# Attention scores on two halves of the rows, S5 in crosswise groups, another order at the ends of the MLPs, and a retuned schedule

## The chip, the cores and the metric

One core of one Trainium2 chip. The metric is the device time of one execution in microseconds. Three executions of the kernel before took 1063.42, 1063.46 and 1065.54 us; the median is 1063.46.

## The reference, cut to what matters

Two residual layers on x of 512 tokens by 1024, float32, each followed by a squared-ReLU MLP (1024 to 4096 and back), every part with an RMS norm ahead and behind. Layer 0 mixes by S5 (32 groups of 16 channels, 64 complex states) and by attention with forget gates (8 heads of 64); layer 1 by pooling and by a spatial gating unit.

```python
def s5_mixer(u, lam_re, lam_im, log_dt, b_re, b_im, c_re, c_im, d, w_glu):
    ...                                   # a = exp(lam dt), bb = q b
    bu = einsum('lbgh,gph->lbgp', ut, bb)             # complex
    x = associative_scan(x_t = a x_{t-1} + bu_t)      # over the tokens
    y = gelu(Re(x c) + d * u)
    return y * sigmoid(y @ w_glu)

def fox_attention(q, k, v, f_logit, b_f):
    F = cumsum(log_sigmoid(f_logit + b_f), axis=1)
    # per block i of 128 queries:
    s = einsum('bqhd,bkhd->bhqk', qi, k) * Dh ** -0.5 + (F_q - F_k)
    p = softmax(where(k_pos <= q_pos, s, -inf))
    return einsum('bhqk,bkhd->bqhd', p, v)

def sq_relu_mlp(h, w1, w2):
    return square(relu(h @ w1)) @ w2

for l in range(2):
    x = x + rms_norm(mixer_l(rms_norm(x)))
    x = x + rms_norm(sq_relu_mlp(rms_norm(x), w1[l], w2[l]))
```

## The kernel before

Every engine call is recorded by a `Program` (`record`), and at the end `issue` puts the recorded operations into an order for each engine: a list scheduler runs a model of the engines with costs from `cost`, and takes of the ready operations the one with the best priority. The priority comes from the place in the record and from labelled bonuses in the table `BOOST`; `LOOKS` and `RANK` set how far ahead of the oldest operation an engine may look, `STICKY` favours a bank of PSUM that is already being accumulated. Buffers and banks are given out in that order too. All recorded rows of the profile therefore carry one line, L438, and are told apart by their tiles: `b` is a working buffer, `bank` one of the eight banks of PSUM, `ct` the constants, `maskb` and `identb` the causal mask and the identity in bf16. The number behind a name is that of its allocation, and isn't the same in two kernels.

Products in float32 are made of parts: `split` writes a high part (fp32r, by ACT) and the rest (by DVE), and `mm3` multiplies high by high, rest by high and high by rest. A product of 128 rows, 128 outputs and 512 columns is the usual unit.

The mixer of layer 0 is recorded in the order of `ORDER`: f (forget gates), z c t o e (preparation of S5), q0 to q3 (q and k of a pair of heads), u (the S5 input), a0 to a3 (attention of a pair), s0 to s3 (a quarter of S5).

`qk_block` makes q and k of two heads: the product has head 0 on partitions 0 to 63 and head 1 on 64 to 127. Before, four buffers of 1024 columns are filled from it by half-height copies: Q1 and K1 hold for each head both parts stacked on 128 rows, Q2 and K2 the remaining part and, on other rows, the forget terms. `attention` then makes the scores of a head and block with two products of full height (the second 96 or 128 rows) and one product of mask with identity between. The softmax is on DVE and ACT, the probabilities are transposed, and the products with v go to two halves of the columns, one head on each. The blocks come in two phases: (0, 1) and (2, 3).

`step_z` transposes the S5 input matrices in quadrants of 64 x 64 (`ct,b 64*64 64x64` rows). `s5_run` takes a quarter (8 groups): 16 quadrant products W into two banks, complex rotation, two scans and back-rotation on DVE, then one T product and two S products per pair of groups.

The MLP's second product uses a seven-product scheme with the names S1 to S4, A22, X and Z (`Seven`). Its last step, `tail`, works for each half a of the tokens through four groups of 12 matmuls, by (Z, S4), (X, S2), (X, S3), (X, A22). X goes on accumulating while `collect` reads it in between, so the group behind has to wait for that read. When a tile of the output is complete, `post` normalises it, adds it to x, and norms and transposes it for the next layer.

At the start SP issues the loads in the recorded order up to `prog.first`, PE runs 16 warm-up matmuls on `idle`, and the first four tiles of x are normed (`norm_T`) one after another, with rstd computed by two small operations on POOL.

Of the kernel before, what the change touches and what calls it, by code (L numbers as in the profile page):

```python
# [36 lines left out]
LOOKS = {0: (202, 21, 10), 1: (186, 29, 7), 2: (48, 11, 15), 3: (36, 8, 6)}  # L37
HAMT = 3060
POOLF = 1
NWARM = 16  # L40
RANK = 0.55
# [3 lines left out]
PBOOST = 3  # L45
STICKY = 7
# [13 lines left out]
C_ID, C_SEL, C_MASK, C_TRIL, C_IPAD, C_DIAG, C_MISC, C_INV = 0, 128, 256, 384, 512, 736, 752, 768  # L60
C_END = 832


def constants(np):
# [19 lines left out]
    for hd in range(8):  # L84
        c[:, m + 5 + hd] = p % 32 // 4 == hd
    c[:, m + 13] = j >= 2
# [81 lines left out]
class Program:  # L168
# [10 lines left out]
    def __init__(self, engines):  # L179
        self.ops, self.engines, self.rooms = [], engines, []  # L180
        self.shift = 0
        self.boost = 0.0
        self.phase = 0
        self.first = 0

    def record(self, eng, name, args, kw):
# [12 lines left out]
        op.port = eng in ("DVE", "POOL") and name == "tensor_tensor" and not any(v.t.bank for v in ins)  # L199
        if eng == "PE":  # L200
# [6 lines left out]
            op.half = (p0, p0 + outs[0].shape[0]) if ins[0].shape[0] == 128 else (0, 128)  # L207
        for v in ins:
# [36 lines left out]
    def cost(eng, name, outs, ins, args, kw):  # L245
# [8 lines left out]
        if eng == "PE":  # L254
# [7 lines left out]
            if ins[0].t.dt == BF16 or out.shape[0] <= 64:  # L262
                return max(53, cols / 2.4 + 3)
            return max(107, cols / 2.4 + 15)
        if eng == "ACT":
            ptr = sum(isinstance(kw.get(k), View) for k in ("bias", "scale", "accum_out"))
            return 0.833 * n + (67 if psum else 93) + 90 * ptr
        if eng == "DVE":
# [8 lines left out]
            return (0.52 if fast else 1.04) * n + 67 + 64 * ptr  # L277
        if eng == "POOL":
# [4 lines left out]
            if name == "tensor_copy":  # L283
                return 0.83 * n + 180
            return 1.7 * n + 165 + 130 * (name == "tensor_scalar")
        if outs:
            v = outs[0]
            return v.shape[0] * free(v) * 4 / 270.0
        return 1600

    def issue(self):
# [43 lines left out]
        window, work, slow, half = 0, 0.0, 2.0, None  # L335
        events = []
# [19 lines left out]
        while len(order) < total:  # L356
            moved = True
            while moved:
                moved = False
                for e in self.engines:  # L360
# [3 lines left out]
                    for o in avail[e]:  # L364
                        if o.ready <= now and o.wake <= now and not (e == "SP" and head and o is not head[0]):
# [21 lines left out]
                    if e == "SP":  # L387
                        clock[e] = now + 60
                        dma = max(dma, now) + o.ns
                        o.end = dma + 2000  # L390
                    elif e == "PE":
# [3 lines left out]
                        ns = o.ns  # L395
                        if half is not None and (half[1] <= o.half[0] or o.half[1] <= half[0]):
# [145 lines left out]
def tile_trunk(ctx: ExitStack, tc: tile.TileContext, x, mix_pre_g, mix_post_g, mlp_pre_g, mlp_post_g,  # L542
# [431 lines left out]
    class Seven:  # L974
# [55 lines left out]
        def collect(self, row1, c, bank_, a, first=False):  # L1030
            kept = boosted(f"Y{prog.phase}")
# [68 lines left out]
        def tail(self, post, before):  # L1100
# [4 lines left out]
            parts = [[self.part(self.raw[p][1].f(512, 512)) for p in range(4)]]  # L1105
            for p in range(4):
                H, L = self.middle(p)
                parts.append([((H, L), (H.r(0, 512), L.r(0, 512))), ((H, L), (H.r(512, 512), L.r(512, 512)))])
            second, parts = parts[1:], parts[:1]
            parts.append([s_[0] for s_ in second])  # L1110
            parts.append([s_[1] for s_ in second])
            last = []
            for p in range(4):
                r1 = self.raw[p][1]
                last.append(self.part(r1.f(0, 512)))
                r1.free()
            parts.append(last)
# [860 lines left out]
```

## Time and profile before

| | us |
|---|---|
| median of three executions | 1063.46 |
| the profiled execution | 1063.45 |
| its span (first to last instruction) | 1061.7 |
| mean granted clock, as a share of full speed | 0.993 |
| POOL busy | 57.2 |
| DMA, mean over the span | 98 GB/s |

The time of an execution is 1.75 us longer than the span that its instructions take. Rows of the timeline read: start, busy time, engine, line, operation, out<-in, shapes, count, and in brackets the idle time ahead with the engine that ended it. A float32 product on part of the array leaves two records. Rows by group read: line, engine, operation, names and shapes, count, then busy time and mean ns of one, then idle time ahead with its releasers. The layers lie in time so: start to 25 us, layer 0's mixer to 215, its MLP to 585, layer 1's mixer to 730 and its MLP to the end.

### The profile page before, as it was taken

How to read it: one execution, taken by the hardware profiler on the slowest of the kernel's cores; microseconds unless marked ns; L12 is line 12 of the kernel's file. 1: busy time of each engine (PE TensorE's matmuls, PEld its weight loads, DVE VectorE, ACT ScalarE, POOL GpSimd, SP SyncE). 2: the span in 40 equal slices, each digit the busy share in tenths (PEclk: the TensorE clock that was granted, in tenths of full speed). 3: DMA queues.
4: the chain of work that ended last, by engine and by line, in shares of the span. 5: the costliest groups of instructions: out<-in, count | busy, mean ns of one | idle time of the engine just before them, and what ended most of it. 6: DMA issues, size and time to landing. Idle time of an engine off the chain costs nothing.

```text
span 1061.7 us, 13872 instructions
## 1 busy us (share of the span) xinstructions
PE 1039.3 (98%) x5133; PEld 846.6 (80%) x5133; DVE 792.9 (75%) x1365; ACT 568.5 (54%) x1037; POOL 57.2 (5%) x112
## 2 busy tenths in 40 slices
PE   8999899999999999999999799999999999999996
PEld 5789677788988888888888688889888888888885
DVE  6968899759856586677778998566776697686786
ACT  5474978546744563553653644445645544553641
POOL 4001000003000000000001310011000000000001
PEclk9999999999999999999999899999999999999999
DMA  8221012623314322422514533306134225223212
GB/s 254 68 80 40 2 40 81 218 60 119 120 40 131 120 72 66 143 85 78 160 60 132 156 100 113 106 4 198 39 99 121 98 80 164 75 80 120 79 59 80
DMA packets 110385, 104.53 MB, mean 98 GB/s; under 512 B 9736, under 2 KB 92844, under 8 KB 110318
## 3 DMA queue, kind: packets, MB, share of 16 engines
q1 hardware_dynamic: 110318, 103.66, 31.8%
q8 instruction: 40, 0.66, 0.3%
q14 instruction: 27, 0.22, 0.1%
HBM read 101.55 MB, written 2.10 MB: 98 GB/s over the span
## 4 chain that ended last, share of the span: by engine, by line
PE 89%; ACT 5%; DVE 2%; SPq 1%; issue 1%; POOL 1%; DMA 0%; DVEq 0%; POOLq 0%; ACTq 0%
PE bank L438 89%; ACT b L438 5%; DVE b L438 2%; SPq L438 1%; POOL small L438 1%; DMA b<-in_x_dram 0%; ACT junk L438 0%; DVE small L438 0%; POOL b L438 0%; DVEq L1974 0%; POOLq L1974 0%; ACTq L438 0%; ACTq L1974 0%; DVEq L438 0%; POOLq L438 0%
## 5 line engine op out<-in xcount | busy, mean ns | idle before, releaser
L438 PE MATMUL bank<-b,b 128*128 128x512 f32 (+5 forms) x4684 | 1000.2, 376 | 8.9 <-DVE b L438 8.0
L438 PEld LDWEIGHTS bank<-b,b 128*128 128x128 f32 (+2 forms) x4684 | 810.3, 188 | 182.3 <-DVE b L438 7.2
L438 DVE TENSOR_TENSOR b<-b,b 128x1024 fp32r<-128x1024 f32 (+7 forms) x654 | 483.2, 775 | 128.8 <-ACT b L438 65.2
L438 ACT ACTIVATE b<-b 128x1024 fp32r<-128x1024 f32 (+6 forms) x582 | 376.1, 690 | 261.3 <-DVE b L438 121.9
L438 ACT ACTIVATE b<-bank 128x512 f32<-128x512 f32 (+7 forms) x269 | 131.3, 516 | 148.4 <-PE bank L438 138.2
L438 DVE TENSOR_TENSOR b<-bank,b 128x512 f32<-128x512 f32 (+2 forms) x210 | 120.7, 604 | 50.9 <-PE bank L438 30.9
L438 DVE TENSOR_TENSOR b<-b 128x256 f32<-128x256 f32 (+5 forms) x202 | 91.0, 466 | 36.0 <-PE bank L438 23.9
L438 POOL TENSOR_SCALAR small<-small 128x1 f32<-128x1 f32 x36 | 15.9, 443 | 852.9 <-ACT junk L438 836.7
L438 ACT ACTIVATE junk<-b 128x512 bf16<-128x512 f32 (+1 forms) x32 | 27.0, 843 | 43.5 <-DVE b L438 37.0
L438 PE MATMUL bank<-ct,b 128*128 128x128 f32 (+3 forms) x387 | 43.0, 260 | 5.0 <-DVE b L438 4.5
L438 DVE SCALAR_TENSOR_TENSOR b<-b,small,b 128x1024 f32<-128x1024 f32 (+1 forms) x32 | 36.4, 1150 | 14.8 <-POOL small L438 14.8
L438 PEld LDWEIGHTS bank<-ct,b 128*128 128x128 f32 (+3 forms) x387 | 33.9, 140 | 15.9 <-DVE b L438 6.1
L438 DVE SCALAR_TENSOR_TENSOR b<-b,b 128x512 f32<-128x512 f32 (+2 forms) x28 | 19.0, 686 | 13.9 <-ACT b L438 13.5
L438 POOL TENSOR_TENSOR small<-small,mhalf 128x1 f32<-128x1 f32 x36 | 26.7, 741 | 2.9
L438 ACT ACTIVATE b<-bank,small 128x128 f32<-128x128 f32 (+4 forms) x36 | 19.2, 545 | 7.4 <-DVE small L438 4.5
L438 ACT ACTIVATE junk<-bank 128x512 bf16<-128x512 f32 x16 | 9.5, 594 | 23.3 <-PE bank L438 23.0
L438 DVE TENSOR_REDUCE small<-bank 128x1 f32<-128x128 f32 (+3 forms) x32 | 14.0, 484 | 2.2 <-PE bank L438 2.0
L438 DVE SCALAR_TENSOR_TENSOR b<-b,bank 128x512 f32<-128x512 f32 x16 | 10.9, 681 | 4.8 <-ACT b L438 4.7
L438 POOL MEMSET b<- 128x4 f32 (+4 forms) x27 | 9.2, 375 | 78.7 <-ACT b L438 26.5
L438 DVE TENSOR_SCALAR b<-b,small 128x128 f32<-128x128 f32 (+3 forms) x28 | 9.9, 376 | 1.3 <-POOL small L438 1.1
L438 DVE TENSOR_TENSOR_SCAN b<-b,b 128x512 f32<-128x512 f32 x8 | 9.8, 1221 | 0.2
L438 POOL CAST b<-b 32x512 fp32r<-32x512 f32 (+1 forms) x8 | 5.3, 663 | 65.3 <-ACT b L438 64.9
(41 smaller groups left out, 97.8 us busy)
## 6 DMA issues: line engine op xcount, KB each, us to landing
b<-in_mlp_w_dram SPq DMA_DIRECT2D x128, 512.0 KB, 4.4
b<-in_w_in_even_dram SPq DMA_DIRECT2D x16, 512.0 KB, 6.7
b<-in_w_in_odd_dram SPq DMA_DIRECT2D x12, 512.0 KB, 4.2
b<-in_w_out_even_dram SPq DMA_DIRECT2D x8, 512.0 KB, 3.5
b<-in_w_out_odd_dram SPq DMA_DIRECT2D x8, 512.0 KB, 3.5
b<-in_x_dram SPq DMA_DIRECT2D x7, 512.0 KB, 5.3
out_dram<-b SPq DMA_DIRECT2D x8, 256.0 KB, 2.0
b<-in_s_w_glu_dram SPq DMA_DIRECT2D x2, 512.0 KB, 3.7
```

The source lines that it names most:

```text
L438: o.ins = o.fn(*args, **kw)
```

## The change

Scheduler: the tables `LOOKS`, `RANK`, `STICKY`, `PBOOST` and all of `BOOST` get new values; a penalty `MODE` is added for a PE operation whose array mode differs from the last one's; `cost` gets new figures (an SP issue 440 instead of 60, ACT and DVE operations on fewer than 128 partitions, POOL copies, short rows of a DMA); a pair of products on different row halves counts as one. So the order of nearly everything differs. `prog.hold` makes POOL operations that are recorded behind the first norms wait for those.

Attention: q and k are split at full height, and the forget terms get a buffer F of their own. The masks of a phase come first, then four products for each head and block (three of q and k, one of forget terms), on 64 rows for each head.

S5: the pairs of groups lie crosswise (columns j, g, e), step z uses full transposes, and the W products of one bank alternate between the two columns of U and V; DVE works on 1024 columns where it had 512, and the T products come ahead of the S products. `tail` of the MLP takes (X, S2) first; its collects carry the label E. At the start, weights are loaded ahead of the S5 tables, and x's third and fourth tile ahead of most tables.

```diff
-LOOKS = {0: (202, 21, 10), 1: (186, 29, 7), 2: (48, 11, 15), 3: (36, 8, 6)}
+LOOKS = {0: (68, 32, 16), 1: (282, 37, 15), 2: (7, 29, 6), 3: (33, 35, 7)}
-RANK = 0.55
+RANK = 0.5000000000000001
-PBOOST = 3
-STICKY = 7
+PBOOST = 0
+STICKY = 2
+MODE = 9
...
+        if self.hold is not None and self.hold.eng == eng:
+            op.preds[id(self.hold)] = self.hold
...
+                            if e == "PE" and o.narrow != narrow:
+                                key += MODE * 1e3
...
-                for n, (bank_, which) in enumerate(((Z, S4), (X, S2), (X, S3), (X, A22))):
+                for n, (bank_, which) in enumerate(((X, S2), (Z, S4), (X, S3), (X, A22))):
...
+                    if n == 0:
+                        self.collect(1, 1, X, a, label="E")
                     if n == 1:
-                        self.collect(1, 1, X, a)
...
                     if n == 2:
-                        self.collect(0, 1, X, a)
+                        self.collect(0, 1, X, a, label="E")
...
-    prog.first = len(prog.ops)
-    SP.dma_start(lam.f(0, 128, slice(0, 16)), lam_re[0].rearrange("(r g) p -> r (g p)", g=2))
...
     for _ in range(3):
         load_w()
+    SP.dma_start(lam.f(0, 128, slice(0, 16)), lam_re[0].rearrange("(r g) p -> r (g p)", g=2))
...
     load_x0(2)
     load_x0(3)
+    prog.first = len(prog.ops)
...
+    prog.hold = [o for o in prog.ops if o.eng == "POOL"][-1]
...
-                for k in range(8):
-                    for H in HALF:
-                        PE.matmul(ps[H, 64 * k:64 * k + 64], z.f(512 * q + 64 * k, 64, H), ident[H, H],
-                                  start=True, stop=True)
+                for k in range(4):
+                    transpose(ps[:, 128 * k:128 * k + 128], z.f(512 * q + 128 * k, 128))
...
-        for r in range(4):
-            pr = 4 * cb + r
-            for H in HALF:
+        for j in range(2):
+            for g, H in enumerate(HALF):
                 for n in range(2):
-                    PE.matmul(W_[n][H, 128 * r:128 * r + 128], Vst[n].f(64 * pr, 64, H),
-                              U[cb // 2].f(128 * (pr % 8), 128, H), start=True, stop=True)
+                    for e_, E_ in enumerate(HALF):
+                        PE.matmul(W_[e_][H, 256 * n + 128 * j:256 * n + 128 * j + 128],
+                                  Vst[n].f(128 * (2 * cb + j) + 64 * g, 64, E_),
+                                  U[cb // 2].f(128 * ((4 * cb + 2 * j + g) % 8), 128, E_), start=True, stop=True)
...
-        for hb in range(2):
-            hd, p = 2 * hp + hb, PF[hb]
-            act(Q2.r(512 * hb, 512, p), fsel.f(0, 512, p), AF.Identity, scale=mc(5 + hd, p), bias=mst[p, hd:hd + 1])
-            KF(K2.r(512 * hb, 512, p), fmov.r(0, 512, p))
+        products = [(Q.r(a, 512), K.r(b, 512)) for a, b in ((0, 0), (512, 0), (0, 512))] + [(F.r(), fmov.r())]
...
+            for i in blocks:
+                for hb in range(2):
+                    PE.matmul(view(hb, i)[:, 128 * i:128 * i + 128], identb, maskb, start=where[i][1] == 0, stop=False,
+                              skip_group_check=True)
...
-                for hb in range(2):
-                    o = 512 * hb
-                    PE.matmul(pss[hb], Q1.r(o, 512)[:, qs], K1.r(o, nk), start=True, stop=False)
-                    PE.matmul(pss[hb][:, nk - 128:nk], identb, maskb, start=False, stop=False)
-                    PE.matmul(pss[hb], Q2.r(o, 512, PB[hb])[:, qs], K2.r(o, nk, PB[hb]), start=False, stop=True)
+                pss = [view(hb, i) for hb in range(2)]
+                for n, (L, R) in enumerate(products):
+                    for hb, H in enumerate(HALF):
+                        PE.matmul(pss[hb], L[H, qs], R[H, 0:nk], start=False, stop=n == 3, skip_group_check=True)
...
-            for o, H, L in ((0, lo, hi), (512, hi, lo)):
-                if q:
-                    act(K1.r(o, 512, H), ps[H], AF.Copy)
-                    act(K1.r(o, 512, L), ps[H], AF.Copy)
-                    sub(K2.r(o, 512, H), ps[H], K1.f(o, 512, H))
-                else:
-                    act(Q1.r(o, 512, H), ps[H], AF.Copy, scale=0.125)
-                    act(Q2.r(o, 512, H), ps[H], AF.Copy, scale=0.125)
-                    stt(Q1.r(o, 512, L), ps[H], 0.125, Q1.f(o, 512, H), ALU.mult, ALU.subtract)
-        QK[hp] = qk
+            split(ps, *(qk[q].r(o, 512) for o in (0, 512)), scale=None if q else 0.125)
+        F = alloc_r(512)
+        act(F.r(), fsel.f(), AF.Identity, scale=ct[:, C_HEAD + hp:C_HEAD + hp + 1],
+            bias=ct[:, C_HEAD + 4 + hp:C_HEAD + 5 + hp])
+        QK[hp] = qk + [F]
```

What this makes of the order, at three places of PE. First the scores of the first pair of heads, before (a row names the bank, the moving and the stationary tile; `b74`, `b73` are K1 and Q1, `b76`, `b75` are K2 and Q2; one bank for each head and block):

```order
L438 MATMUL bank4_815<-b74_582,b73_527 128x384
L438 LDWEIGHTS identb_115
L438 MATMUL bank4_815<-maskb_271,identb_115 128x128
L438 MATMUL bank4_815<-b76_602,b75_543 128x384
L438 MATMUL bank5_820<-b74_582,b73_527 128x512
L438 LDWEIGHTS identb_115
L438 MATMUL bank5_820<-maskb_271,identb_115 128x128
L438 MATMUL bank5_820<-b76_602,b75_543 128x512
```

Now, the second pair (`b133` is K, `b132` Q, `b55` the moving forget terms, `b140` F; head 0 goes to `bank3`, head 1 to `bank0`; eight masks stand ahead):

```order
L463 MATMUL bank3_1331<-b133_1317,b132_1311 128x128 x2
L463 MATMUL bank0_1334<-b133_1317,b132_1311 128x128
L463 MATMUL bank3_1331<-b133_1317,b132_1311 128x128
L463 MATMUL bank0_1334<-b133_1317,b132_1311 128x128
L463 MATMUL bank3_1331<-b55_796,b140_1272 128x128
L463 MATMUL bank0_1334<-b133_1317,b132_1311 128x128
L463 MATMUL bank0_1334<-b55_796,b140_1272 128x128
```

Each head has four products instead of two, the mask has left the place between them, and the heads alternate but for the first and last two of a block. In the first pair the alternation is looser (`b74`, `b73` are K and Q, `b81` F; `bank3` and `bank6` are the two heads of block 3, `bank4` one head of block 2; the last two rows are transposes of probabilities):

```order
L463 MATMUL bank3_808<-b74_625,b73_502 128x512
L463 MATMUL bank6_814<-b74_625,b73_502 128x512
L463 MATMUL bank3_808<-b55_796,b81_802 128x512
L463 MATMUL bank6_814<-b74_625,b73_502 128x512
L463 MATMUL bank6_814<-b55_796,b81_802 128x512
L463 LDWEIGHTS identb_105
L463 MATMUL bank4_858<-maskb_288,identb_105 128x128
L463 MATMUL bank4_858<-b74_625,b73_502 128x384 x3
L463 MATMUL bank4_858<-b55_796,b81_802 128x384
L463 MATMUL bank7_872<-ct_67,b82_836 128x128
L463 MATMUL bank7_872<-ct_67,b84_844 128x128 x2
```

One head's block stands by itself at the end, four products in a row, and the transposes follow it at once. The third place is the end of layer 0's MLP. Before (`bank_5002` is X in its last group, A22; `bank_5348` and `bank_5353` take the transposes of the second normed tile, `bank_5391` and `bank_5404` those of the third):

```order
L438 MATMUL bank_5002<-b_5183,b_5130 128x512
L438 MATMUL bank_5337<-ct,b_5179 128x4
L438 MATMUL bank_5348<-ct,b_5340 128x128 x4
L438 MATMUL bank_5353<-ct,b_5340 128x128 x4
L438 MATMUL bank_5002<-b_4795,b_4785 128x512 x2
L438 MATMUL bank_5002<-b_4795,b_4802 128x512
L438 MATMUL bank_5002<-b_5030,b_4912 128x512 x2
L438 MATMUL bank_5391<-ct,b_5381 128x128 x4
L438 MATMUL bank_5404<-ct,b_5381 128x128 x4
L438 MATMUL bank_5002<-b_5030,b_4930 128x512
```

Now (`bank_4910` is X, at the end of A22; `bank_5323` is the first product of layer 1, and `bank_5341` and `bank_5346` take the second tile's transposes):

```order
L463 MATMUL bank_4910<-b_5151,b_5089 128x512
L463 MATMUL bank_5323<-b_5201,b_5250 128x512
L463 MATMUL bank_5323<-b_5210,b_5250 128x512
L463 MATMUL bank_5323<-b_5201,b_5265 128x512
L463 MATMUL bank_5323<-b_5201,b_5250 128x512
L463 MATMUL bank_5323<-b_5210,b_5250 128x512
L463 MATMUL bank_5323<-b_5201,b_5265 128x512
L463 MATMUL bank_5323<-b_5218,b_5258 128x512
L463 MATMUL bank_5323<-b_5299,b_5258 128x512
L463 MATMUL bank_5323<-b_5218,b_5272 128x512
L463 MATMUL bank_5341<-ct,b_5329 128x128 x4
L463 MATMUL bank_5346<-ct,b_5329 128x128 x4
```

The transposes of the second tile have moved from ahead of A22 to behind A22 and nine matmuls of the next layer.

More of the change, by code (lines that the diff above doesn't have):

```diff
@@ L83, in constants @@
     c[32:, m + 4] = np.where(j == 3, -1.0, 0.0)[32:]
-    for hd in range(8):
-        c[:, m + 5 + hd] = p % 32 // 4 == hd
-    c[:, m + 13] = j >= 2
+    for hp in range(4):
+        own = np.where(p < 64, p % 32 // 4 == 2 * hp, (p < 96) & (p % 32 // 4 == 2 * hp + 1))
+        c[:, C_HEAD + hp] = own
+        c[:, C_HEAD + 4 + hp] = own & (j >= 2)
     for g, w in enumerate(WINDOWS):
@@ L184, in __init__ @@
         self.first = 0
+        self.hold = None
     def record(self, eng, name, args, kw):
@@ L197, in record @@
         op.ns = self.cost(eng, name, outs, ins, args, kw)
-        op.port = eng in ("DVE", "POOL") and name == "tensor_tensor" and not any(v.t.bank for v in ins)
+        op.port = (eng == "DVE" and name == "tensor_tensor" and not any(v.t.bank for v in ins)) or (eng == "POOL" and ins != [])
         if eng == "PE":
@@ L207, in record @@
             op.half = (p0, p0 + outs[0].shape[0]) if ins[0].shape[0] == 128 else (0, 128)
+            k0, k = ins[0].region()[0], ins[0].shape[0]
+            op.narrow = name == "matmul" and (ins[0].dtype == F32 and outs[0].shape[0] <= 64 or k == 64)
+            op.rows = k0 if k == 64 and outs[0].shape[0] == 128 else None
+            op.turn = name == "transpose"
         for v in ins:
@@ L287, in cost @@
             v = outs[0]
-            return v.shape[0] * free(v) * 4 / 270.0
+            src = ins[0].ap if ins and not isinstance(ins[0], View) else args[1].ap
+            row = src[-1][1] * 4 if src[-1][0] == 1 else 4
+            return v.shape[0] * free(v) * 4 / min(270.0, 0.36 * row)
         return 1600
@@ L335, in issue @@
         window, work, slow, half = 0, 0.0, 2.0, None
+        narrow = turn = False
+        rows = None
         events = []
@@ L387, in issue @@
                     if e == "SP":
-                        clock[e] = now + 60
+                        clock[e] = now + 440
                         dma = max(dma, now) + o.ns
-                        o.end = dma + 2000
+                        o.end = dma + (4500 if now < 12e3 else 2000)
                     elif e == "PE":
@@ L395, in issue @@
                         ns = o.ns
+                        if o.narrow != narrow:
+                            ns, narrow = ns + 125, o.narrow
+                        elif turn and not o.turn:
+                            ns -= 60
+                        turn = o.turn
+                        if rows is not None and o.rows is not None and o.rows != rows:
+                            ns, rows = 10, None
+                        else:
+                            rows = o.rows
                         if half is not None and (half[1] <= o.half[0] or o.half[1] <= half[0]):
@@ L1028, in begin, with collect @@
                     self.collect(0, 1, self.Z, c, True)
-        def collect(self, row1, c, bank_, a, first=False):
-            kept = boosted(f"Y{prog.phase}")
+        def collect(self, row1, c, bank_, a, first=False, label="Y"):
+            kept = boosted(f"{label}{prog.phase}")
             y = self.yp[2 * a + row1].f(512 * c, 512)
@@ L1104, in tail @@
             arena.reserve = RESERVE
[L1105 removed]
+            parts = [[], [], [], []]
             for p in range(4):
+                parts[1].append(self.part(self.raw[p][1].f(512, 512)))
                 H, L = self.middle(p)
[L1108 to L1112, printed above, removed]
+                parts[0].append(((H, L), (H.r(0, 512), L.r(0, 512))))
+                parts[2].append(((H, L), (H.r(512, 512), L.r(512, 512))))
             for p in range(4):
                 r1 = self.raw[p][1]
[L1115 removed]
+                parts[3].append(self.part(r1.f(0, 512)))
                 r1.free()
[L1117 removed]
             before()
             for a in range(2):
[L1120 removed]
+                for n, (bank_, which) in enumerate(((X, S2), (Z, S4), (X, S3), (X, A22))):
                     for p in range(4):
@@ L1320, in tile_trunk @@
     wv = [getw() for _ in range(4)]
+    bt = alloc(512)
+    for o, src in ((0, b_re), (256, b_im)):
+        SP.dma_start(bt.f(o, 256).rearrange("p (r h) -> p r h", r=16),
+                     src[0].rearrange("(r g) p h -> (g p) r h", g=2))
+    craw = alloc(512)
+    for o, src in ((0, c_re), (256, c_im)):
+        SP.dma_start(craw.f(o, 256).rearrange("p (t q) -> p t q", t=4),
+                     src[0].rearrange("(t g) h p -> (g h) t p", t=4))
+    dbc = alloc(512)
+    SP.dma_start(dbc.f(0, 512, HALF[0]), s5_d[0].partition_broadcast(64))
     vtok = [alloc(1024) for _ in range(NT // 2)]
```

113 lines of the change are left out of this document (51 added, 62 removed), and 10 rows, old and new, of the table BOOST.

## The prediction

> **What bounds the kernel now.** I read the page first (busy time, slices, chain), then a table of stretches, then the waits of PE one by one.
>
> ```profile
> span 1061.7 us, 13872 instructions
> PE 1039.3 (98%) x5133; PEld 846.6 (80%) x5133; DVE 792.9 (75%) x1365; ACT 568.5 (54%) x1037; POOL 57.2 (5%) x112
> PE   8999899999999999999999799999999999999996
> PE 89%; ACT 5%; DVE 2%; SPq 1%; issue 1%; POOL 1%; DMA 0%; DVEq 0%; POOLq 0%; ACTq 0%
> ```
>
> TensorE is busy 98% of the span and carries 89% of the chain that ends last; the other engines have room. So there are two ways to win: give PE less to do, or close its 22.4 us of idle time (1061.7 less 1039.3). The low digits of the slices say where the idle time lies: the start, the first fifth, the middle and the end. The table of stretches (length, then busy PE, PEld, DVE, ACT, POOL with counts, the granted clock, the DMA share, GB/s):
>
> ```profile
> 0.00:12.00 12.00, 10.03 (x33) 4.41 (x33) 3.95 (x12) 5.71 (x13) 8.44 (x20) 1.00 0.76 250
> 12.00:25.00 13.00, 11.86 (x53) 8.87 (x53) 11.80 (x46) 7.90 (x19) 1.87 (x5) 1.00 0.99 248
> ...
> 55.00:95.00 40.00, 38.82 (x301) 34.69 (x300) 26.84 (x82) 25.17 (x57) 3.60 (x5) 1.00 0.24 65
> 95.00:130.00 35.00, 32.33 (x244) 25.17 (x241) 30.63 (x63) 26.31 (x68) 3.33 (x11) 0.99 0.06 16
> 130.00:160.00 30.00, 28.87 (x191) 22.13 (x192) 27.56 (x57) 22.75 (x49) 0.21 (x2) 0.96 0.12 36
> 160.00:215.00 55.00, 54.44 (x335) 41.46 (x334) 45.53 (x89) 38.25 (x78) 0.21 (x2) 1.00 0.48 158
> ...
> 260.00:570.00 310.00, 310.00 (x1420) 255.43 (x1420) 223.83 (x329) 159.97 (x263) 0.00 (x0) 1.00 0.31 96
> 570.00:600.00 30.00, 24.39 (x109) 19.74 (x108) 25.61 (x36) 17.54 (x32) 6.72 (x15) 0.89 0.60 175
> 600.00:730.00 130.00, 130.00 (x647) 109.08 (x646) 98.50 (x149) 58.51 (x107) 18.22 (x28) 1.00 0.34 106
> 730.00:1040.00 310.00, 310.00 (x1389) 254.92 (x1388) 224.61 (x332) 161.72 (x266) 1.07 (x2) 1.00 0.29 90
> ```
>
> The MLP of layer 0 (260 to 570) and all of layer 1 but its end (600 to 1040) have no gap: nothing is to be won there by another order. The mixer of layer 0 (55 to 215) loses 1.18 + 2.67 + 1.13 + 0.56 = 5.5 us, the passage from layer 0 to layer 1 (570 to 600) 5.6. The single waits behind these sums, and the clock after two of them:
>
> ```profile
> 59.40 1.16 PE L438 MATMUL bank<-b,b 128*128 128x512 f32 x3 [1.18 <-DVE b L438]
> 129.82 4.38 PE L438 MATMUL bank<-b,b 128*128 128x128 f32 x23 [2.67 <-DVE b L438]
> 588.07 1.09 PE L438 MATMUL bank<-ct,b 128*128 128x128 f32 x8 [2.25 <-DVE b L438]
> 592.51 2.50 PE L438 MATMUL bank<-b,b 128*128 128x512 f32 x5 [3.36 <-DVE b L438]
> 1051.44 3.06 PE L438 MATMUL bank<-b,b 128*128 128x512 f32 x12 [0.79 <-DVE b L438]
> 129.80:132.50 2.70, 2.68 (x10) 2.51 (x11) 2.66 (x4) 2.65 (x4) 0.04 (x1) 0.50 0.00 0
> 593.00:596.40 3.40, 3.40 (x14) 2.81 (x13) 3.40 (x4) 2.18 (x4) 0.00 (x0) 0.50 0.65 186
> ```
>
> Each time PE waits for DVE, and behind the two long waits the granted clock is 0.50 for 2.7 and 3.4 us, which costs half of that again: 1.35 and 1.7 us. So the mixer can give back 5.5 + 1.35 = 6.9 us, the passage 5.6 + 1.7 = 7.3, the end 0.8, the start some 2 to 3.
>
> All sums below are made against the profiled execution: 1063.45 us, of which 1061.7 are the span. It lies 0.01 below the median of the three runs.
>
> **The scores.** Four rows of one head pair in before, at the full block (512 keys):
>
> ```profile
> 68.97 0.23 PE L438 MATMUL bank<-maskb,identb 128*128 128x128 bf16 x1
> 69.01 0.71 PE L438 MATMUL bank<-b,b 96*128 96x512 f32 x2
> 69.56 0.23 PE L438 MATMUL bank<-maskb,identb 128*128 128x128 bf16 x1
> 320.00:360.00 40.00, 40.00 (x175) 32.41 (x174) 21.74 (x31) 17.36 (x28) 0.00 (x0) 1.00 0.35 106
> ```
>
> The last row is the rate where nothing waits: 175 matmuls in 40 us, 0.23 each for 512 columns, 0.45 ns a column. From 68.97 to 69.01 the mask takes 0.04; from 69.01 to 69.56 two products of 512 columns take 0.55 instead of 0.46, so the product behind a mask pays another 0.09. A mask thus costs 0.13, and 32 of them 4.1 us. The products: per head pair four of each of 128, 256, 384 and 512 columns, at 0.11 (short ones run at the price of a transpose, below), 0.12, 0.18 and 0.23, that is 4 x 0.64, times four pairs 10.3. Together 14.4 us.
>
> After the change a head has four products a block on its 64 rows, 128 in all, head 0 on the upper half of the rows and head 1 on the lower. No row of before shows two row halves on the same columns. The nearest rows are the pairs on two halves of the columns, and the quadrants of S5:
>
> ```profile
> 75.39 0.60 PE L438 MATMUL bank<-ct,b 128*128 128x128 f32 x4
> 75.92 0.87 PE L438 MATMUL bank<-b,b 128*64 128x256 f32 x8
> 76.72 0.65 PE L438 MATMUL bank<-ct,b 128*128 128x128 f32 x4
> 96.81 1.96 PE L438 MATMUL bank<-b,b 64*64 64x128 f32 x32
> ```
>
> Eight records of products on column halves take 0.80 (75.92 to 76.72), 0.10 each with up to 256 columns, which alone is 0.12 and more; and 32 records of quadrants take 1.96, 0.06 each, less than the 0.11 of a whole tile of that width. Halves of the array run side by side there. Bounds for the 128 products: 10.3 if every product finds a partner, 20.6 if none does. Between them lies what the order allows. The order rows of the second pair read A A B A B A B B for the two heads; if a matmul starts only when its predecessor has started, only neighbours of different heads overlap, and walking the four pairs that way gives 4.1 + 3.0 + 3.5 + 3.0 = 13.7 (the first is worst: its rows have three of one head in a row). Nothing in the trace shows a matmul that overtook an earlier one, so I take 13.7. The masks now stand together: 32 x 0.04 = 1.3; changing from whole tiles to halves costs 0.09 (four transposes take 0.53 from 75.39 to 75.92 instead of 0.44), so entering and leaving four times 0.7, say 0.8. Together 15.8, which is +1.4 us, between -2.0 and +8.3.
>
> The Trainium skill, "TensorE: Matmul & The Clock Gate", Part 3: Packing small matmuls, says of row groups that they run concurrently, but also that matmuls are strictly first in, first out in start and end. That speaks against the order above, which doesn't alternate the heads; by that rule the sum is the one I took, and without it 3.4 us lower. The rows above don't decide, since their neighbours alternate anyway.
>
> **S5.** Step z transposed 64 quadrants, now 16 full tiles:
>
> ```profile
> 54.01 4.21 PE L438 MATMUL bank<-ct,b 128*64 128x128 f32 x110
> 580.68 1.03 PE L438 MATMUL bank<-ct,b 128*128 128x128 f32 x8
> ```
>
> The first row is nearly all of the step, 4.0 us to its last start; eight full transposes take 0.87 to their last end less a drain, 0.11 each, so sixteen take 1.75. That is -2.2 us, between -2.0 and -2.9 (the step at most 4.7 long). The 64 quadrant products W keep their number, but each column half now comes twice in a row. Where the halves overtake nothing, 16 products of a block take nine steps of 0.22 (two records of 0.11) instead of eight: +0.9 for four blocks; between 0 and +3.9 (25 half steps for 16, if the two passes of a product stay together). DVE loses two operations a block, ACT gains eight short copies; no PE row waits for those copies now.
>
> **The waits of the mixer.** The q and k halves cost ACT and DVE this much before:
>
> ```profile
> L438 ACT ACTIVATE b<-bank 64x512 fp32r<-64x512 f32 x32 | 18.9, 592 | 9.5 <-PE bank L438 6.0 <-issue 3.1
> L438 DVE SCALAR_TENSOR_TENSOR b<-bank,b 64x512 fp32r<-64x512 f32 x8 | 5.5, 689 | 1.2 <-ACT b L438 1.0
> L438 DVE TENSOR_TENSOR b<-bank,b 64x512 fp32r<-64x512 f32 x8 | 5.5, 685 | 0.2
> ```
>
> After: 8 ACT copies at full height (4.7 us by the 592 ns), 8 DVE operations (5.5). So ACT loses 14 us, DVE 5.5, in a stretch where DVE is 87% to 92% busy (95 to 160) and PE waits for DVE each time. The 129.82 wait stands right there; less DVE work ahead of it makes it shorter by what lies in its own stage, a quarter to a half of the 5.5. The new order also puts the forget chain behind more PE work (the wait at 59.40). New waits can arise, since the first head pair now comes earlier. I take half of the 6.9: -3.5, between -6.9 and +3.
>
> **The passage to layer 1.** DVE's rows between the two waits of before:
>
> ```profile
> 588.77 1.28 DVE L438 SCALAR_TENSOR_TENSOR b<-b,small,b 128x1024 f32<-128x1024 f32 x1 [0.76 <-POOL small L438]
> 589.98 1.22 DVE L438 TENSOR_TENSOR b<-b,b 128x1024 fp32r<-128x1024 f32 x1
> 591.11 2.01 DVE L438 TENSOR_TENSOR b<-bank,b 128x256 fp32r<-128x256 f32 x5
> ```
>
> PE's 3.36 at 592.51 is product A22, which writes the bank that the collect of S3 must first read; the collect is the last of the five at 591.11. Ahead of it DVE normalises a tile (1.28), splits a weight (1.22) and four halves. By the order rows of after, A22 follows S3 without transposes between, and its collect has a raised priority of its own: behind S3's end remain the rest of one 1.28, one 1.22 and the collect 0.69, about 2.85. Then 12 matmuls of A22 and 9 of v, 4.8 us, cover most of the second tile, whose transposes wait some 0.7. Idle 3.55 instead of 5.6 and a little, so -2.1 to -2.4, and up to -4.1 if the clock stays up. I take -3.3, the middle; 0 if another operation takes the collect's place in DVE's queue.
>
> **Start and end.** The loads of x2 and x3 now go ahead of the S5 tables on SP, and POOL's clearing of buffers no longer stands ahead of the first norm:
>
> ```profile
> 24.89 0.63 PE L438 MATMUL bank<-ct,b 128*128 128x128 f32 x4 [0.48 <-DVE b L438]
> ```
>
> POOL, on which the first norm's two small steps run, is busy 8.44 of the first 12 us, mostly with clearing; the wait at 24.89 is the last tile of x. With DMA 0.99 busy from 12 to 25 the weights remain, so only part of the 1.97 + 1.14 us goes: -1.0, between -2.5 and +1. At the end the last collect stands first on DVE, some 0.25 of the 0.79: -0.3. Elsewhere (260 to 570, 600 to 1040) PE has no gap and DVE is idle for 28% of it, which hides what is moved there: 0. If that cover went, a wait there would cost as at 592.51, 3.4.
>
> **Sum.** +1.4 - 2.2 + 0.9 - 3.5 - 3.3 - 1.0 - 0.3 = -8.0: 1063.45 - 8.0 = 1055.5 us.
>
> **The rivals.** First, the heads find partners in any order. Scores 12.4 and W +0: 4.3 less, 1051.2. For it: quadrants and column halves run side by side. Against: no row in which a matmul overtook another. 0.17.
>
> Second, the row halves don't run side by side at all, since they use the same columns of the array, which no row shows. Scores 22.7 instead of 15.8: 1062.4, no change. 0.12.
>
> Third, the order only moves the waits. The -8.1 of waits (3.5 + 3.3 + 1.0 + 0.3) falls away: 1063.6, no change. The change then does not do what its new tables are to do. For it: DVE stays 80% busy where PE waits. 0.13.
>
> Fourth, slower: the softmax of a head pair loses its cover. Between the last scores of a phase and the transposes of its probabilities the order of the first pair has no other matmul. If DVE's chain is later than PE there, each pair costs a wait as at 129.82 with its clock, 2.67 + 1.35 = 4.0; from two pairs on the gain of 8.0 is gone, with four the time is 1055.5 + 16 = 1071.5. Against: pair one's earlier blocks were scored well before. 0.10.
>
> My forecast's case has 0.48. **Range:** from the best of rival one (1051.2 with the waits at their better end, some 4 lower) to the second and third rivals: 1047 to 1064; the slower case is left out. A measurement of this kernel can tell about 0.2% (2.1 us) from no change. Faster: the forecast's case nearly whole, rival one, and a bit of two: 0.70; same 0.18; slower 0.12.
>
> **What would show it.** Scores: sum of starts over the 128 products, 10, 14 or 21 us, and whether records of the two heads start within 0.01 of each other. Step z: sixteen transposes in under 2 us. The waits: one row each at the forget chain, at the S5 products near 130, and two near 585; a granted clock of 0.50 behind any is its second half. I am wrong if PE's idle time stays near 22 us, if a new row with over 2 us of idle stands in the first 215 us, or if the products of one head never start beside the other's.

## The result, and the profile after

The change takes the kernel from 1063.44 to 1052.15 us (medians of four runs each, 1063.07 to 1065.54 and 1051.40 to 1052.69). The ratio is 0.989, 95% interval 0.9878 to 0.9903. The profiled execution took 1051.40 us, its span 1049.6: 12.1 us less than the span of before. It is the shortest of its four runs, so the differences of traces below are up to 0.8 us larger than those of medians.

The page of the changed kernel, the lines that answer to those of before:

```profile
span 1049.6 us, 13707 instructions
PE 1031.5 (98%) x5085; PEld 842.7 (80%) x5085; DVE 785.8 (75%) x1348; ACT 554.3 (53%) x1017; POOL 48.8 (5%) x104
PE   8999999999999999999999999999999999999996
PE 89%; DVE 7%; ACT 1%; POOL 1%; issue 1%; DMA 1%; SPq 0%; DVEq 0%; POOLq 0%; ACTq 0%
```

The 7 in the middle of the PE line is gone. PE idles 18.1 us instead of 22.4 (1049.6 less 1031.5), and is busy 7.8 us less. Its table of stretches, with limits that follow the same stages some 10 us earlier:

```profile
0.00:12.00 12.00, 9.93 (x34) 4.47 (x34) 4.30 (x9) 6.27 (x15) 2.60 (x10) 1.00 0.83 271
12.00:25.00 13.00, 11.70 (x61) 9.28 (x61) 12.58 (x48) 9.24 (x23) 4.00 (x10) 1.00 0.95 248
...
55.00:95.00 40.00, 40.00 (x258) 34.72 (x258) 32.32 (x102) 23.22 (x64) 1.06 (x2) 1.00 0.20 53
95.00:130.00 35.00, 33.95 (x238) 28.25 (x237) 34.48 (x70) 21.10 (x58) 0.21 (x2) 1.00 0.10 31
130.00:160.00 30.00, 26.65 (x227) 20.41 (x226) 25.07 (x55) 22.57 (x54) 0.42 (x4) 1.00 0.22 71
160.00:205.00 45.00, 44.99 (x274) 34.71 (x273) 28.55 (x50) 24.66 (x48) 0.53 (x5) 1.00 0.42 140
...
560.00:590.00 30.00, 28.34 (x131) 22.52 (x130) 26.52 (x35) 14.57 (x27) 7.77 (x13) 1.00 0.67 198
590.00:720.00 130.00, 129.34 (x656) 108.30 (x655) 102.30 (x158) 63.09 (x113) 12.72 (x31) 1.00 0.36 110
```

Idle time of PE, before and after: start 3.1 and 3.4 us; mixer of layer 0 5.5 and 4.4; passage to layer 1 5.6 and 2.3 (1.66 + 0.66). And the granted clock is 1.00 in every one of these rows. Before had two stretches at 0.50. They are longer than the 2.7 and 3.4 us that the prediction read, since its two windows lay inside them; cut at their edges and at the end of each wait, they read:

```profile
129.26:129.80 0.54, 0.00 (x0) 0.01 (x1) 0.54 (x2) 0.53 (x2) 0.07 (x1) 0.50 0.00 0
129.80:132.67 2.87, 2.85 (x11) 2.68 (x12) 2.83 (x4) 2.82 (x4) 0.04 (x1) 0.50 0.00 0
590.06:592.50 2.44, 0.00 (x0) 0.00 (x0) 2.44 (x5) 2.35 (x5) 0.79 (x2) 0.50 0.55 150
592.50:596.88 4.38, 4.37 (x14) 3.75 (x15) 4.38 (x6) 2.97 (x6) 0.00 (x0) 0.50 0.71 205
```

So PE worked for 2.85 and 4.37 us at half clock, which cost half of that, 1.4 and 2.2 us. The waits that are left in the changed kernel:

```profile
117.14 0.22 PE L463 MATMUL bank<-maskb,identb 128*128 128x128 bf16 x1 [0.67 <-DVE b L463]
...
131.60 1.80 PE L463 MATMUL bank<-b,b 128*128 128x128 f32 x14 [1.26 <-POOL b L463]
134.12 0.66 PE L463 MATMUL bank<-ct,b 128*128 128x128 f32 x4 [0.72 <-ACT b L463]
...
579.27 5.12 PE L463 MATMUL bank<-b,b 128*128 128x512 f32 x21 [1.58 <-DVE b L463]
...
1039.10 3.01 PE L463 MATMUL bank<-b,b 128*128 128x512 f32 x12 [0.55 <-DVE b L463]
```

No wait is over 1.6 us; before had 1.2, 2.7, 2.3 and 3.4. Of PE's work, the groups by form show W (quadrants of 64 x 64, 128 columns) and step z in before:

```profile
L438 PE MATMUL bank<-b,b 64*64 64x128 f32 x128 | 9.4, 275 | 0.0
L438 PE MATMUL bank<-ct,b 64*64 64x64 f32 x128 | 4.3, 220 | 0.0
```

In the changed kernel step z has become 16 of the full transposes, W has the same count, and the products on row halves are new:

```profile
L463 PE MATMUL bank<-b,b 64*64 64x128 f32 x128 | 7.3, 279 | 0.1
L463 PE MATMUL bank<-b,b 64*128 64x384 f32 x32 | 5.6, 342 | 0.0
L463 PE MATMUL bank<-b,b 64*128 64x512 f32 x32 | 5.3, 393 | 0.0
```

Summed from each start to the next, waits taken off: W 8.7 before and 7.2 after; step z 4.2 and 1.75; the scores' 128 products 13.5, and with the masks and the changes of array form 16.3, against the 14.4 worked out for before (14.6 by the same sum in before's trace); full transposes other than step z's 28.5 and 25.9; the products with v and others on column halves 18.5 and 17.6. So the 12.1 us of span come from **idle time 4.3**, **half clock 3.6** (1.4 and 2.2) and **PE work about 4.2**, which is what remains. Up to 1.1 of the 4.2 is chance: the 16 warm-up products took 5.9 us in before's trace and 4.8 in this one, and between 4.8 and 6.3 in the eight other traces below that share its start (the old tail and every run from step z on).

### The profile page after: what moved, and what is told of

The parts are those of the page before. It is cut to its first block, busy times and chain, and to the rows that moved or that the text cites. A ratio compares the mean times of both kernels' runs of the same rounds, so it can differ in the third digit from the quotient of the medians.

```text
span 1049.6 us, 13707 instructions
## 1 busy us (share of the span) xinstructions
PE 1031.5 (98%) x5085; PEld 842.7 (80%) x5085; DVE 785.8 (75%) x1348; ACT 554.3 (53%) x1017; POOL 48.8 (5%) x104
## 4 chain that ended last, share of the span: by engine, by line
PE 89%; DVE 7%; ACT 1%; POOL 1%; issue 1%; DMA 1%; SPq 0%; DVEq 0%; POOLq 0%; ACTq 0%
PE bank L463 89%; DVE b L463 6%; ACT junk L463 1%; POOL small L463 1%; DMA b<-in_w_in_even_dram 1%; DVE small L463 1%; ACT b L463 1%; SPq L463 0%; DVEq L1987 0%; POOLq L1987 0%; POOL b L463 0%; ACTq L1987 0%; DVEq L463 0%; ACTq L463 0%
## 5 line engine op out<-in xcount | busy, mean ns | idle before, releaser
L463 PE MATMUL bank<-b,b 128*128 128x512 f32 (+7 forms) x4748 | 998.0, 375 | 5.5 <-DVE b L463 3.1
L463 PEld LDWEIGHTS bank<-b,b 128*128 128x128 f32 (+4 forms) x4748 | 807.6, 187 | 179.6 <-issue 8.6
L463 DVE TENSOR_TENSOR b<-b,b 128x1024 fp32r<-128x1024 f32 (+9 forms) x646 | 481.5, 782 | 112.8 <-ACT b L463 52.3
L463 ACT ACTIVATE b<-b 128x1024 fp32r<-128x1024 f32 (+7 forms) x582 | 378.7, 690 | 226.4 <-DVE b L463 114.7
L463 ACT ACTIVATE b<-bank 128x512 f32<-128x512 f32 (+6 forms) x253 | 118.1, 498 | 185.1 <-PE bank L463 179.9
L463 DVE TENSOR_TENSOR b<-b 128x256 f32<-128x256 f32 (+6 forms) x202 | 90.9, 462 | 32.3 <-PE bank L463 15.6
L463 PE MATMUL bank<-ct,b 128*128 128x128 f32 (+2 forms) x275 | 39.4, 274 | 2.9 <-DVE b L463 1.7
L463 PEld LDWEIGHTS bank<-ct,b 128*128 128x128 f32 (+2 forms) x275 | 31.5, 139 | 12.3 <-DVE b L463 3.9
L463 DVE SCALAR_TENSOR_TENSOR b<-b,b 128x512 f32<-128x512 f32 (+2 forms) x28 | 19.2, 686 | 18.7 <-ACT b L463 18.5
L463 POOL TENSOR_TENSOR small<-small,mhalf 128x1 f32<-128x1 f32 x36 | 22.7, 631 | 3.0
L463 DVE SCALAR_TENSOR_TENSOR b<-b,small,bank 128x512 f32<-128x512 f32 x8 | 5.9, 745 | 4.0 <-PE bank L463 3.9
```

The lines of the kernel that those rows point to most:

```text
L463: o.ins = o.fn(*args, **kw)
```

## The experiments

Two theories were held against each other. **A**: the waits went because the order of the queues is better, and PE's work (z, W) is on the path. **B**: they went because the split at full height takes 14 us off ACT and 5.5 off DVE in the mixer. All times are medians; before took 1063.98 to 1064.39 us beside these runs.

### One part of the change undone, the schedule made anew

The S5 part, the attention, the MLP's tail and the start were put back to the code of before, one at a time, with the new tables; and the tables and cost model alone. The core of each edit:

```diff
 u_attn
-            split(ps, *(qk[q].r(o, 512) for o in (0, 512)), scale=None if q else 0.125)
+                    act(K1.r(o, 512, H), ps[H], AF.Copy)
+                    act(K1.r(o, 512, L), ps[H], AF.Copy)
...
 u_s5
-                    transpose(ps[:, 128 * k:128 * k + 128], z.f(512 * q + 128 * k, 128))
+                        PE.matmul(ps[H, 64 * k:64 * k + 64], z.f(512 * q + 64 * k, 64, H), ident[H, H],
...
 u_tail
-                for n, (bank_, which) in enumerate(((X, S2), (Z, S4), (X, S3), (X, A22))):
+                for n, (bank_, which) in enumerate(((Z, S4), (X, S2), (X, S3), (X, A22))):
...
 u_head
-    prog.hold = [o for o in prog.ops if o.eng == "POOL"][-1]
...
 u_sched
-LOOKS = {0: (68, 32, 16), 1: (282, 37, 15), 2: (7, 29, 6), 3: (33, 35, 7)}
+LOOKS = {0: (202, 21, 10), 1: (186, 29, 7), 2: (48, 11, 15), 3: (36, 8, 6)}
```

> The changed kernel with the attention of before (Q1, K1, Q2, K2, mask between two full-height products, half-height copies), all else as changed. Theory A (the split scores cost PE time: 16.3 us with masks in the changed trace, 14.4 worked out for before; what they give is 14 us of ACT and 5.5 us of DVE in the mixer): PE's score work falls by about 2 us, waits on DVE in 55 to 215 us rise by 1 to 4 us, time 1051 to 1055. Rival B (the relief of DVE and ACT is the main gain of the whole change): waits in the mixer rise by 5 us or more, time 1057 or above.

> The changed kernel with S5's layout of before (64 quadrant transposes in step z, W products in diagonal quadrants, twelve DVE operations in a quarter). Theory A: z returns 2.4 us and W 1.5 us of PE time, all of it on the path since PE is the bound there: 1056 (1055 to 1058). Rival B: the mixer's waits take up the difference, time within 1 us of 1052.

> The changed kernel with the MLP's tail of before (Z, S4 first, collects without a label of their own). Theory A: the waits at the passage to layer 1 come back in part, 1.6 us of idle becomes 3 to 5 and the granted clock may drop behind it: 1053.5 to 1057. Rival B: the passage was mended by the new table of priorities alone, time within 0.7 us of 1052.

> The changed kernel with the start of before (S5 tables ahead of weights and of x's last tiles in SP's order, POOL's clearing free to go ahead of the first norm). Theory A: PE's idle time in the first 25 us hardly differs between the two kernels (3.1 and 3.4 us), so the start gives little: 1051.5 to 1054. Rival B: the start's gain is hidden in work done earlier (the last tiles of x are normed 6 us earlier in the changed kernel), time 1055 or above.

> The changed kernel with the tables and the cost model of before (the array-mode penalty gone as well), all else as changed. Theory A (tables and program only fit together, as the parts undone one by one showed): waits of 10 us or more in the mixer, time 1060 to 1085. Rival B (the parts bring their gain whatever the tables, the tables theirs): 1055 to 1059.

| undone | us | ratio to before, 95% interval |
|---|---|---|
| attention | 1067.07 | 1.0025 (1.0014 to 1.0036) |
| S5 | 1075.05 | 1.0099 (1.0079 to 1.0119) |
| tail | 1057.67 | 0.9939 (0.9924 to 0.9953) |
| start | 1081.29 | 1.0159 (1.0142 to 1.0176) |
| tables and cost model | 1086.97 | 1.0218 (1.0201 to 1.0236) |

Four of the five are slower than before, which has none of the parts; attention and start land where rival B put them and the tables near theory A, but for reasons of neither, and S5 above both. The undone start shows why. PE idles 3.7 us in its first 25, little more than the change's 3.4, but this row of its timeline stands in the mixer:

```profile
147.05 0.88 PE L460 MATMUL bank<-ct,b 128*128 128x128 f32 x3 [5.75 <-DVE b L460]
```

A wait of 5.8 us, 120 us behind the edit. The scheduler makes a new order for the whole program from every edit, and these tables give a good one for this program and hardly another. So such a run measures the tables' fit, not the part; its total says nothing on what the part is worth. Only the undone tail leaves the mixer as it was, and can be read: two rows of its timeline, at the passage and at the end,

```profile
579.13 5.18 PE L463 MATMUL bank<-b,b 128*128 128x512 f32 x15 [3.39 <-DVE b L463]
1043.50 3.02 PE L463 MATMUL bank<-b,b 128*128 128x512 f32 x12 [0.96 <-DVE b L463]
```

where the change has 1.58 and 0.55. The tail's order is worth these 2.2 us. Behind the longer wait the clock is at 0.50 until 582.29, which costs another 1.6 in this trace, and the 5.5 between the medians go with the clock too: its four executions took 1055.34, 1057.27, 1058.07 and 1058.99 us with mean clocks of 0.997, 0.995, 0.994 and 0.990.

### One cost put back, every queue's order held

From here on the schedule is computed for the changed kernel and only what an entry sends is altered. First step z:

```diff
                     transpose(ps[:, 128 * k:128 * k + 128], z.f(512 * q + 128 * k, 128))
+                    prog.ops[-1].fn = quadrants
```

> The changed kernel with every queue's order held: only step z's 16 full transposes are sent as 64 quadrant transposes, at the same place. They land in the old places, so S5's input matrices are not the reference's and neither is the output. Theory A (PE's work is on the path there): step z takes about 4.0 us instead of 1.75, time 2.2 us longer, 1054.4. Rival B (later waits of the mixer take it up): the waits at 117, 131, 134 and 138 us shrink instead, time within 0.8 us of 1052.2.

1056.42 us (1054.84 to 1057.52). The 64 quadrants appear (128 records, 4.4 us busy), the waits behind them are those of the change (at 121, 136, 138 and 142 us), so nothing takes the work up: theory A. The profiled execution is the slowest of the four, its span 5.9 us longer than the change's: 1.3 are lost ahead of the edit, at the start (PE is that much later at 44 us), 2.9 between 44 and 68 us, where the quadrants stand, and 1.6 in one row of its table of stretches, where the clock fell with PE fully busy:

```profile
160.00:164.00 4.00, 4.00 (x15) 2.74 (x14) 3.26 (x9) 2.63 (x8) 0.00 (x0) 0.59 0.00 0
```

Next, the half-height copies and differences of q and k:

```diff
 h_relief
+            prog.ops[-2].fn = halves(prog.ops[-2].fn, (0, 0, 1, 1))
+            prog.ops[-1].fn = halves(prog.ops[-1].fn, (0, 1))
 h_relief2: the second two pieces of a copy go to a spare buffer
+            for dest in (o, spare.real()):
+                for H in HALF:
+                    fn(dest[H], a[H], f, **k)
 h_dve: only the differences
+            prog.ops[-1].fn = halves(prog.ops[-1].fn)
```

> The changed kernel with every queue's order held: only the copies and differences of q and k are sent in half-height pieces again, each ACT copy as four and each DVE operation as two, with the same values. ACT gets about 14 us more, DVE 5.5 us, all in the mixer of layer 0. Theory A: 1 to 4 us of it reach PE as waits, 1053 to 1056. Rival B (this relief is the main gain): 1057 or more. Rival C (PE's cover hides it): within 0.8 us of 1052.2.

> As the run that sends q's and k's copies and differences in half-height pieces with every order held, but the second two pieces of each ACT copy go to a spare buffer, so that DVE's difference waits only for two pieces of 0.59 us instead of one of 0.61, not for four. The same added work (14 us of ACT, 5.5 us of DVE) without the added wait on DVE's queue. Theory B (the relief is a main gain of the change): at least half of the 20.8 us stays, 1062 or more. Theory A (most of the 20.8 us was DVE blocked behind the longer copies): 1053 to 1058.

> The changed kernel with every order held; only the differences of q and k (DVE) are sent as two half-height pieces each, 5.5 us more on DVE in the mixer. Theory B: DVE is the bound in the stretches around 117 and 131 to 139 us, the added 0.7 us apiece reach PE there: 1054 to 1058. Theory A: covered, within 0.8 us of 1052.2.

| put back | us | ratio to before, 95% interval |
|---|---|---|
| ACT and DVE pieces | 1072.93 | 1.0077 (1.0060 to 1.0093) |
| the same, spare buffer | 1071.32 | 1.0069 (1.0054 to 1.0084) |
| DVE pieces only | 1061.23 | 0.9976 (0.9965 to 0.9987) |

Theory B holds, and by more than it said: 5.5 us of DVE work cost 9.1, all of the pieces 19.2. Longer copies ahead of DVE's difference were not the reason, since the spare buffer gives back only 1.6. The run with DVE pieces alone, its table of stretches and three of its waits:

```profile
112.00:122.00 10.00, 7.44 (x49) 5.95 (x49) 9.91 (x18) 4.70 (x12) 0.00 (x0) 0.97 0.00 1
121.00:125.00 4.00, 4.00 (x32) 3.30 (x30) 3.46 (x10) 3.02 (x10) 0.00 (x0) 0.57 0.00 0
...
141.00:149.00 8.00, 7.08 (x28) 4.03 (x28) 7.68 (x18) 4.85 (x12) 0.10 (x1) 0.57 0.14 57
119.12 0.23 PE L463 MATMUL bank<-maskb,identb 128*128 128x128 bf16 x1 [1.37 <-DVE b L1753]
120.55 0.23 PE L463 MATMUL bank<-maskb,identb 128*128 128x128 bf16 x1 [1.19 <-DVE b L1753]
...
141.92 0.90 PE L463 MATMUL bank<-ct,b 128*128 128x128 f32 x3 [1.34 <-DVE b L463]
```

DVE is busy 9.91 of 10 us where PE starts to wait, at the added operations themselves (L1753). PE's idle time rises from 18.1 to 21.2 us, and behind the waits it works at 0.57 for 12 us: 3 us of waiting and 5 of half clock make most of the 9. In the run with the spare buffer one wait is 5.56 us long, and 11.7 us behind it run at 0.50.

Then the scores at full height, two products for each head and block instead of four on half the rows:

```diff
                         PE.matmul(pss[hb], L[H, qs], R[H, 0:nk], start=False, stop=n == 3, skip_group_check=True)
+                        prog.ops[-1].fn = full(L[:, qs], R[:, 0:nk]) if n in (0, 3) else lambda *a, **k: None
```

> The changed kernel with every queue's order held: two of the four score products of a head and block are left out, the other two run at full height, 128 rows, so that the scores are not the reference's. Theory A: the split on two row halves costs PE more than it saves; scores and masks take 12 to 13 us instead of 16.3, time 1048.5 to 1050. Rival B: the softmax on DVE is the bound in that stage, waits take up the difference, time within 0.8 us of 1052.2.

1052.48 us (1051.21 to 1053.40): no change, the time of rival B. The second pair's scores take 2.65 us (118.31 to 120.96) against the change's 2.74 (117.89 to 120.63): where the two heads find partners, halves cost no more than full height. In the first pair full height saves about 1 us, and the next transposes wait for the softmax instead:

```profile
72.20 1.19 PE L1687 MATMUL bank<-b,b 128*128 128x256 f32 x5 [0.18 <-ACT b L463]
...
74.56 0.55 PE L463 MATMUL bank<-ct,b 128*128 128x128 f32 x3 [0.53 <-DVE b L463]
```

But waits explain only a part. In this trace scores and masks take 13.2 us, 3.1 less than in the change, and PE's idle time rises by 1.8 (19.9 for 18.1). The rest is hidden by two things that need not come from the edit: the warm-up products took 6.3 us instead of 4.8, and the clock was at 0.50 from 157.2 to 160.6 us, 1.7 more. So rival B's reason is shown for about 1.8 of the 3.1 us only.

### How far PE looks for a partner

The order of the score products alone, inside each run of them: one head's block after the other's (A A A A B B B B), or strictly by turns.

```diff
 s_block
+                new = [o for t in seen for o in run if o.banks[0] is t]
 s_alt
+                a = [o for o in run if o.rows == run[0].rows]
+                b = [o for o in run if o.rows != run[0].rows]
+                new = [o for p in zip(a, b) for o in p] + a[len(b):] + b[len(a):]
```

> The changed kernel with the order of the score products changed alone: of each run of them, all four of one head and block stand together, then all four of the other head (A A A A B B B B instead of A A B A B A B B). If PE looked any distance ahead for a product of the idle row half, the scores would take the same 13.5 us and the time 1052.2; if it looks past one waiting product at most (what the changed trace suggests: full pairs in the second to fourth head pair, single file in the first), they take 18 to 20 us. Theory with the result of the full-height run (waits hide score work): of these 5 us, 1 to 4 show, 1053 to 1056.

> The changed kernel with the order of the score products changed alone: within each run the two row halves strictly alternate. The first head pair's stretch from 69.6 to 73.9 us, 4.3 us, should fall to about 3.4, those of the others (2.75 for the second) stay. Time 1051 to 1052.5, better than the change by less than can be told if DVE's softmax waits take it up.

By blocks: 1055.02 us (1053.81 to 1055.27); the products take 14.4 us, not 18 to 20, against 13.5 in the change; in the trace, waits add 1.4 us more and a half clock from 75.6 to 79.0 another 1.7. By turns: 1053.30 us (1052.33 to 1054.39), products 12.9; the first pair's stretch with its masks falls from 4.3 to 3.7 us, and the time doesn't follow, in a trace that has a half clock of its own (156.9 to 160.3 us, 1.7). No run is clearly shorter than the changed kernel.

In the run by blocks the second pair's order is four products A of 128 columns, four A of 256, then four B of 128. The tile's answer for two windows of its trace (count, durations, first and last start, forms):

```profile
L486 PE MATMUL bank<-b,b x4: 271/272/322, 120.7 to 121.1; 64*128 64x128 f32 x4
...
L486 PE MATMUL bank<-b,b x7: 270/278/328, 121.1 to 121.5; 64*128 64x128 f32 x4, 64*128 64x256 f32 x3
```

Up to 121.10 the four short ones of A start, one by one. The first B of 128 columns starts at 121.216, 6 ns behind A's first of 256 at 121.210, while A's other three of 256 are still to come (121.379, 121.497 and 121.616). A product on the idle half of the rows thus passed three waiting ones, and no more: it didn't start with A's fourth. In the first pair, nine A ahead of B, the first B starts 7 ns behind A's sixth: three again. The third and fourth pairs, in the order of the second, show the same (153.056 and 153.063; 178.099 and 178.106). In these four places the count of three falls together with A's change to wider products; in the third pair of the changed kernel it doesn't: head 1's first product of 512 columns starts at 150.966, 6 ns behind head 0's third of 384, with a fourth of 384 and two of 512 still waiting.

A partner within reach is not enough when it waits for another engine. In the first pair of the changed kernel seven products of head 0 run alone from 70.20 us on, and head 1's first product of 256 columns starts only at 71.24. In the program that product waits for ScalarE, and ScalarE's first exponential in this stretch ends at 71.19:

```profile
70.73 0.37 ACT L463 ACTIVATE b<-bank,small 128x128 f32<-128x128 f32 x1 [3.26 <-DVE small L463]
71.00 0.19 ACT L463 ACTIVATION_READ_ACCUMULATOR b<-bank,small 128x1 f32 x1
```

## Why the prediction was right, and where it was not

The forecast was 1055.5 with 1047 to 1064; measured 1052.15, 3.4 us below. The sum of the terms came out 3 to 4 us short, and three of them fell as reasons. That the sum still came so near is in part luck: W and the passage gave some 2.3 us more each than forecast, the mixer and the start 1.0 less each, and work that had no term moved as well.

- **Scores, +1.4.** The trace gives +1.9 (16.3 for 14.4; +1.7 against before's trace), and the products 13.5 for 13.7, but by luck: not by the step as put, that a matmul starts only when its predecessor has started. PE passes up to three waiting products, so pairs two and four run nearly without gaps (2.74 us) in the order that was to cost 3.0, while the first and third, where a block of one head stands alone, take 4.4 and 3.6 instead of 4.1 and 3.5. In the first pair the wait for ScalarE at 71.24 adds to it, which the walk didn't have. The Trainium skill's rule in "TensorE: Matmul & The Clock Gate", Part 3: Packing small matmuls, that matmuls start in strict order, does not hold in these records; that row groups run concurrently does. And how much of the term is time was not settled: of 3.1 us less (full height), waits gave back 1.8, and the clock hid the rest.
- **Step z, -2.2.** The trace gives -2.45; put back with the order held it costs 4.3 between the medians. In the trace it costs 2.9 where it stands, and 1.6 is clock.
- **W, +0.9.** Wrong in sign: -1.5. The same rule failed. Records of all four quadrants start within 0.03 us of each other; 32 products of two blocks take 2.6 us, where before took 1.9 for 16. Before used the two diagonal quadrants alone, so that two products could run at once; the crosswise layout uses all four, which the walk of nine steps left out.
- **Mixer's waits, -3.5.** Idle time fell by 1.1 and the half clock by 1.4: 2.5. The runs that put DVE's and ACT's work back show that the changed order needs the relief, not that the relief is what shortened the waits of before. Its size was taken as a quarter to a half of the 5.5 us; with the order held it is more than all of it. What it would have been worth under the order of before was not measured.
- **Passage, -3.3.** Idle time fell by just that (5.6 to 2.3), and the half clock went too, 2.2 more (forecast from 1.7): 5.5. The walk gave 2.85 + 0.7 us of waits; they are 1.58, 0.08 and 0.50. The run with the old tail shows the tail's part as 1.8 of it.
- **Start, -1.0.** Nothing in idle time (3.1 and 3.4 us). The last tile's wait at 24.89 went, others came. The shorter warm-up is not the change's, as said above.
- **End, -0.3.** 0.79 to 0.55: as walked.

What the sum lacked is some 3.5 us of transposes and of products on column halves (2.6 and 0.9 in the sums above). They have the same count and stand in another order; 0.7 of it is the half clock of before (eight transposes between 593.0 and 596.4 take 1.56 us, at 0.11 each they would take 0.88), and why the rest fell is open. Against it the products of 512 columns outside the scores, the half clock taken off, take some 2 us more, which is open too. Of the rivals, the first (partners in any order) comes nearest with 1051.2: its mechanism was right up to three places. Its number is luck too: it had scores and masks at 12.4 us, and they take 16.3.

## What to carry to other kernels

Where a list scheduler's tables are fitted to one program, undoing a part and scheduling anew measures the fit; hold the order and alter only what an entry sends. A stretch in which one engine is 98% busy and the main engine waits is where work taken off that engine can pay more than its own length, since here the clock halved behind the waits (5.5 us put back cost 9.1); of work taken off the main engine, waits can take a part back (1.8 of 3.1 us). Read a change of waits together with the granted clock behind them, and take the edges of the half clock from the trace: here 4.3 us of idle time brought 3.6 us of clock with it. Where single executions differ by as much as the part in question, look in the trace for what the clock did ahead of and behind the edit before the difference is put down to it.

## What the runs showed of the hardware

PE lets a product on the free half of the rows pass three waiting products of the other half, and no more, in the five places where it was counted. The half clock, away from the end of the kernel, lasts 3.41 us or a multiple of it: 3.41 and 6.83 in before (129.26 to 132.67, 590.06 to 596.88), 3.41 with the old tail (578.87 to 582.29), 13.65 with the spare buffer (144.18 to 157.83). It can begin while PE waits: in before 0.54 and 2.44 us of it lie ahead of the end of the wait. It comes not only behind long waits: with step z put back, at full height and by turns it lay at the same place of the program (159.8, 157.2 and 156.9 us), each time with PE fully busy throughout; in the 4 to 7 us ahead PE had waited for 0.3, 1.3 and 0.3 us in all. And it differs between executions of one kernel: the old tail's four executions span 3.7 us with mean clocks of 0.997 to 0.990. What sets it off was not settled.
